# A one-core encoder layer: score corrections over all 128 rows with zeros, and weight chunks placed by their use

## The chip, the cores and the metric

The kernel runs on one core of a Trainium2 chip. A core has TensorE (PE), VectorE (DVE), ScalarE (ACT), GpSimd (POOL) and SyncE (SP), each with its own instruction stream, and they meet through semaphores. The metric is the device time of one execution, in microseconds. All that is told of the hardware here is read from this kernel's trace.

## The reference

The reference is one layer of a hybrid encoder on x of 512 positions by 1024 channels, all in float32. One projection gives q, k, v for differential attention (8 heads, two softmax maps each) and z, x, B, C, dt for a Mamba-2 scan in both directions (16 heads, 4 groups). Both results are concatenated, projected, added to the residual and normalized; then a SwiGLU of width 2816 and a second norm follow.

```python
h = x @ w_in                                    # q, k, v, z, xbc, dt
s = einsum(q, k) * scale - slopes * dist        # two maps c per head
p = softmax(s); a = p[:, :, 0] - lam * p[:, :, 1]
mix = concat(rmsnorm(a @ v), ssd(z, xbc, dt)) @ w_out
x = layernorm(alpha * x + mix)
x = layernorm(alpha * x + (silu(x @ w_gate) * (x @ w_up)) @ w_down)
```

## The kernel before

PE multiplies in float32r. Each float32 operand is split in two parts, h (the value rounded by a copy on ACT) and l (the rest, a subtraction on DVE), and `mm3` (line 174) takes three products: h h, h l, l h. The 130 weight chunks of 128 x 1024 pass through a ring: `wload` brings one by DMA into one of three raw buffers, `wprep` (line 101) makes its two parts `wh` and `wl`, `wget` keeps two chunks ahead. The output projection's and the down projection's last four chunks stay resident (`hold`, `keep`) instead.

Which operand moves differs by stage. For q, k and the convolved columns (`col_units`) the chunk is the stationary operand and x^T (`xh`, `xl`) moves, 512 columns at a time. For z and v (`row_units`) x^T is stationary and the chunk moves, 256 columns at a time. In the SwiGLU, a 2 x 2 Winograd scheme per pair of column tiles (`p_1` to `p_7`, 12 products of 256 columns each, line 887), the weights are stationary; blocks A11 and A12 come from the ring, the sums S1 to S4 and A22 from other tiles. In the output and the down projection the chunk moves, 512 columns.

The stages follow each other: a start (loading and splitting x, dt and decays, first convolution), the scan of four SSD groups into which z and the next group's projections are woven, the attention of eight heads into which the next projections are woven by the hand-written counts HEAD_FILL, the output projection, the norm, the SwiGLU, the down projection. PE's order within a stage is made from this by a scheduler; the listing does not show it.

A head's scores work thus. Q's parts are stacked in `QS`: for map c=0 rows 0 to 63 hold the h part and rows 64 to 127 the l part, for c=1 the other way. `KS` holds K's h part twice, so one product over 128 rows gives Qh Kh + Ql Kh (line 590). What is missing is Qh Kl: `kl` holds K's l part on rows 0 to 63 for c=0 and on 64 to 127 for c=1, and the correction (line 592) multiplies only the 64 rows where QS has the h part. There are 8 heads x 4 tiles x 2 maps = 64 scores and 64 corrections. Each map has its own score bank, two in all. After both, DVE adds the distance penalty and takes a minimum (line 595), ACT the exponential (line 598), then transposes and the product with v follow.

Of the kernel before, what the change touches and what calls it, by code (L numbers as in the profile page):

```python
# [8 lines left out]
F32 = mybir.dt.float32  # L9
# [4 lines left out]
P = 128  # L14
# [36 lines left out]
def encoder(ctx, tc, xt, xs, wall, wdt, consts, masks, vecs, pvec, lnv, out):  # L51
# [21 lines left out]
    def weave(steps, units, counts):  # L73
        """Emits steps in order with counts[i] of the units after step i, and the remaining units at the end."""
        done = 0
        for f, n in zip(steps, counts, strict=True):
            f()
            for u in units[done:done + n]:
                u()
            done += n  # L80
        for u in units[done:]:
            u()

# [1 line left out]
    cst = cp.tile([P, N_C], F32, name="cst")  # L85
# [6 lines left out]

    wcache = {}
    AHEAD = 2

    def wload(i):
# [4 lines left out]
    def wprep(i, raw=None, h=None, l=None):  # L101
        raw = wload(i) if raw is None else raw
        if h is None:
            h = wp.tile([P, 1024], R32, tag="wh", name=f"wh{i}")
            l = wp.tile([P, 1024], R32, tag="wl", name=f"wl{i}")
        A.copy(h, raw)  # L106
        V.tensor_tensor(l, raw, h.bitcast(F32), op=ALU.subtract)  # L107
        wcache[i] = (h, l)
# [6 lines left out]

# [1 line left out]
    xh = xtp.tile([P, KT, S], R32, tag="xh", name="xh")  # L117
# [6 lines left out]
    with tc.tile_pool(name="xraw", bufs=1) as xr:  # L124
# [30 lines left out]
        for k in range(KT):  # L155
            T.matmul(dps[0:32], wdp[:, k], xh[:, k], start=False, stop=False)
            T.matmul(dps[0:32], wdp[:, k], xl[:, k], start=False, stop=k == KT - 1)
        dts = ep.tile([32, S], F32, name="dts")
        A.copy(dts, dps[0:32])
# [21 lines left out]
    def col_units(i, name, done, step=2):  # L181
        """x @ w for 128 columns, transposed: [columns, 512]; then done(psum)."""
        st = {}

        def unit(k0):
            if k0 == 0:
                st["o"] = bank("mm", name)
                st["w"] = [w.rearrange("p (k c) -> p k c", k=KT) for w in wget(i)]
            h, l = st["w"]
            mm3(st["o"], [(h[:, k], l[:, k], xh[:, k], xl[:, k]) for k in range(k0, k0 + step)],  # L190
                first=k0 == 0, last=k0 + step == KT)
            if k0 + step == KT:
                done(st["o"])
        return [lambda k0=k0: unit(k0) for k0 in range(0, KT, step)]

    def row_units(i, name, tag, done):
        """x @ w for 256 columns: two banks of [128 positions, 2, 256]; done(half, psum)."""
        st = {}

        def unit(tp, tt, kh):  # L200
            if (tp, tt, kh) == (0, 0, 0):
                w0, w1 = wget(i, 2), wget(i + 1, 1)
                st["w"] = [[w.rearrange("p (k c) -> p k c", k=4) for w in ww] for ww in (w0, w1)]
            if (tt, kh) == (0, 0):
                st["o"] = bank(tag, f"{name}{tp}")
            t = 2 * tp + tt
            sl = slice(t * P, (t + 1) * P)
            h, l = st["w"][kh]
            mm3(st["o"][:, tt * 256:(tt + 1) * 256],
                [(xh[:, 4 * kh + k, sl], xl[:, 4 * kh + k, sl], h[:, k], l[:, k]) for k in range(4)],  # L210
                first=kh == 0, last=kh == 1)
            if (tt, kh) == (1, 1):
                done(tp, st["o"])
        return [lambda a=(tp, tt, kh): unit(*a) for tp in range(2) for tt in range(2) for kh in range(2)]

# [1 line left out]
    sps = ExitStack()  # L217
# [27 lines left out]

# [1 line left out]
    dtv = ep.tile([P, 2, NT, NH], F32, name="dtv")  # L247
    ex = ep.tile([P, 384], F32, name="ex")
    dd = ep.tile([P, 2, 64], F32, name="dd")
    lhsE = ep.tile([P, S], R32, name="lhsE")  # L250
    vals = ep.tile([P, S], F32, name="vals")
    sel = msk[:, M_SEL:M_SEL + 256].rearrange("p (a k) -> p a k", a=2)
    # per direction d: rows erow[d] carry the exponents, the other 64 rows the mask
    erow = (slice(0, 64), slice(64, 128))
# [8 lines left out]
    def decay_steps(dp):  # L263
# [50 lines left out]

        def s1():
            cum = bank("ps", "cum")
            dAf = dA.rearrange("p d t h -> p d (t h)")
# [52 lines left out]

    # stationary parts of the exponents per direction and half of the columns, in the last mix tiles' places
    lhsC = [[mxp[0].tile([P, NT, P], R32, tag=f"m{q}{14 + d}", name=f"lhsC{d}{q}") for q in "hl"] for d in range(2)]
# [6 lines left out]

    # mix^T in two float32r parts: 16 tiles of [128 channels, 512]  # L380
    mixh, mixl = [None] * 16, [None] * 16
# [6 lines left out]

# [1 line left out]
    bc = lambda a, n: a[:, :, None].broadcast_to([a.shape[0], 4, n])  # L390
# [124 lines left out]

# [1 line left out]
    va, qk = {}, {}  # L517

# [9 lines left out]
    def qk_units(h):  # L528
        i = 24 + 6 * (h // 2) + 2 + 2 * (h % 2)
        QS = qp_[h % 2].tile([P, 2, S], R32, tag="QS", name=f"QS{h}")  # L530
        KS = qp_[h % 2].tile([P, 2, S], R32, tag="KS", name=f"KS{h}")
        kl = qp_[h % 2].tile([P, S], R32, tag="kl", name=f"kl{h}")
        qk[h] = (QS, KS, kl)
# [7 lines left out]
        def kdone(o):  # L541
# [4 lines left out]
            for a, b, c in sides:  # L546
                V.tensor_tensor(kl[a], o[a], KS[a, c].bitcast(F32), op=ALU.subtract)
        return col_units(i, f"q{h}", qdone) + col_units(i + 1, f"k{h}", kdone)

# [1 line left out]
    late = []  # L551
# [18 lines left out]

# [1 line left out]
    mxp[0] = mxs.enter_context(tc.tile_pool(name="mxa", bufs=1, side="right"))  # L572

    def head_steps(h, ap):
# [11 lines left out]
        def scores(t):  # L586
            sl = slice(t * P, (t + 1) * P)
            sbs = [bank("s", f"s{h}{t}{c}") for c in range(2)]
            for c in range(2):
                T.matmul(sbs[c], QS[:, c, sl], KS[:, c], start=True, stop=False)  # L590
            for c, r in enumerate((lo64, hi64)):
                T.matmul(sbs[c], QS[r, c, sl], kl[r], start=False, stop=True)  # L592
            for c, sb in enumerate(sbs):
# [51 lines left out]

# [1 line left out]
    def pair(i, ahead=None):  # L647
        return [w.rearrange("p (k c) -> p k c", k=2) for w in wget(i, ahead)]

    def outer_units(i0, order, lhs, acc, n0, n1, total):  # L650
        """acc(t) += lhs tiles (pairs in order) x weight chunks i0 + n0 .. i0 + n1 - 1."""
        st = {}
# [46 lines left out]

# [1 line left out]
    fx = ctx.enter_context(tc.tile_pool(name="fx", bufs=1))  # L701
# [62 lines left out]
    def tile_major(i0, order, lhs, acc, done, hold, after):  # L764
        """As outer_units, with the last NHELD chunks resident and used one sequence tile at a time."""
        n = len(order)
# [21 lines left out]
    acc1 = [[(bank("ps", f"wo1{t}"), 0, 512)] for t in range(NT)]  # L788
    with tc.tile_pool(name="hw", bufs=1) as hw:
        ln1 = ln_consts(hw, 0)  # L790
        tile_major(I_OUT + 8, OUT_ORDER, mix, acc1.__getitem__, done1,
                   lambda j: [hw.tile([P, 1024], R32, tag=f"{q}{j}", name=f"hold{q}{j}") for q in "hl"],
                   lambda: wget(I_FF))
    mxs.close()

# [1 line left out]
    hidp = ctx.enter_context(tc.tile_pool(name="hid", bufs=1, side="right"))  # L797
# [11 lines left out]

    # Winograd's 2 x 2 form: operands from x1^T's blocks B (k half, sequence half)  # L810
    def block(i, j):
# [16 lines left out]
    def t_steps(q):  # L828
        """x1^T of sequence tile 2 + q, and the operands that come of it."""
        b12, b22 = x1t(2 + q, 0), x1t(2 + q, 1)  # L830
# [12 lines left out]

    # operands from the weight blocks of two column tiles: A11 A12 / A21 A22 (columns, k half)
    ops, mats = {}, {}
# [50 lines left out]
    def put(j, f, c, src):  # L896
        """One block of gate (silu) or up (times gate) into hid."""
        d = hid_tile(f)[:, c]
# [46 lines left out]

    # the first two tiles of gate and up, whole; sequence half 0 of three chunks first
    def ff_w(f, w):
# [50 lines left out]

# [1 line left out]
    NEARLY = 1  # L1000
# [5 lines left out]
    def hid_split(e, ph):  # L1006
        """hid tile e in two parts; the later tiles' parts stay for both column halves."""
        key = e if e >= NRING else (ph, e)
# [39 lines left out]
    ffs.close()  # L1048
    dn = ctx.enter_context(tc.tile_pool(name="dn", bufs=1))
    ln2 = ln_consts(dn, 2)  # L1050
    for f in units[NMORE:]:
# [93 lines left out]
```

## Time and profile before

| | us |
|---|---|
| median of 3 runs | 878.93 |
| lowest, highest | 878.69, 879.1 |
| span of the profiled execution | 876.8 |
| PE busy | 862.4 |
| DVE busy | 616.6 |
| ACT busy | 457.7 |
| POOL busy | 121.3 |

The profile gives the span from the first to the last instruction, and no other time of its own execution; the median lies 2.1 us above it. By the timeline the scores run from 237.8 to 443.0 us, the SwiGLU's blocks from some 552 to 752 us. Products overlap in the record: a product of 512 columns is recorded with some 0.39 us, but the next one starts 0.23 us later. To read what a product costs, take the start of one and the start of the next.

### The profile page before, as it was taken

What the parts mean: (1) busy time and instruction counts of PE and PEld (TensorE: products, weight loads), DVE (VectorE), ACT (ScalarE), POOL (GpSimd) and SP (SyncE); (2) the same over time, 40 slices, a digit from 0 to 9 for tenths busy, and PEclk for the clock granted to TensorE, in tenths of its full rate; (3) what the DMA queues carried; (4) which work ended last, traced back from release to release, by engine and by line L of the source; (5) the groups of instructions that cost most, each with busy time, mean ns of one, the idle gap of its engine ahead of it and who ended that gap; (6) DMA issues with size and microseconds to landing.
All of it is one profiled execution on the core that took longest, in us unless ns stands there. A gap on an engine that the chain in (4) does not pass through costs nothing.

```text
span 876.8 us, 13791 instructions
## 1 busy us (share of the span) xinstructions
PE 862.4 (98%) x5404; PEld 748.6 (85%) x5404; DVE 616.6 (70%) x1071; ACT 457.7 (52%) x893; POOL 121.3 (14%) x137
## 2 busy tenths in 40 slices
PE   7999999999999999999999999999999999999996
PEld 3888989899778687786788889999999999888885
DVE  4978788786567666766644579988888887733617
ACT  4777776667456555655632314555555555621500
POOL 3025252535400000000000023000000000000002
PEclk9999999999999999999999999999999999999999
DMA  7321212112212103111135600343233233332402
GB/s 259 113 96 49 73 50 80 66 49 70 76 49 72 50 25 96 50 49 49 49 109 186 209 25 25 112 129 98 96 123 118 98 116 133 112 96 96 145 1 96
DMA packets 23008, 78.74 MB, mean 90 GB/s; under 512 B 2688, under 2 KB 2944, under 8 KB 22944
## 3 DMA queue, kind: packets, MB, share of 16 engines
q1 hardware_dynamic: 22320, 75.60, 25.8%
q0 software_dynamic: 624, 2.27, 0.8%
q8 instruction: 42, 0.69, 0.3%
q14 instruction: 22, 0.18, 0.1%
HBM read 75.77 MB, written 2.10 MB: 89 GB/s over the span
## 4 chain that ended last, share of the span: by engine, by line
PE 67%; DVE 4%; ACT 1%; issue 1%; DMA 0%; POOLq 0%; POOL 0%; DVEq 0%; ACTq 0%
PE M L887 12%; PE N L887 6%; PE dn L178 4%; PE dn L177 4%; PE dn L179 4%; PE wo L177 3%; PE wo L178 3%; PE wo L179 3%; PE C L887 3%; PE o L618 3%; PE s L592 2%; PE s L590 2%; PE at L606 1%; PE v L177 1%; PE k L177 1%; PE q L177 1%
## 5 line engine op out<-in xcount | busy, mean ns | idle before, releaser
L107 DVE TENSOR_TENSOR wl<-wr,wh 128x1024 fp32r<-128x1024 f32 x101 | 124.5, 1233 | 66.8 <-ACT wh L106 63.5
L106 ACT CAST wh<-wr 128x1024 fp32r<-128x1024 f32 x101 | 105.7, 1049 | 77.6 <-PE wo L179 28.6
L598 ACT ACTIVATE ss<-ss,mn 128x512 f32<-128x512 f32 x64 | 46.0, 720 | 25.9 <-DVE mn L595 25.8
L595 DVE CUSTOM_DVE_ANT_0 ss<-s,tab 128x512 f32<-128x512 f32 x64 | 43.2, 688 | 16.4 <-PE s L592 15.8
L178 PE MATMUL dn<-wl,hidh 128*128 128x512 f32 x130 | 51.0, 392 | 0.0
L177 PE MATMUL dn<-wh,hidh 128*128 128x512 f32 x130 | 50.9, 392 | 0.0
L179 PE MATMUL dn<-wh,hidl 128*128 128x512 f32 x130 | 50.6, 389 | 0.0
L893 ACT COPY e<-M 128x256 f32<-128x256 f32 x60 | 22.4, 372 | 43.1 <-PE M L887 43.0
L456 ACT ACTIVATE rE<-vals,msk 64x128 fp32r<-64x128 f32 x128 | 43.0, 391 | 1.0 <-DVE vals L339 0.4
L177 PE MATMUL wo<-wh,mixh 128*128 128x512 f32 x96 | 38.3, 399 | 0.0
L177 PE MATMUL v<-wh,xh 128*128 128x256 f32 x128 | 37.8, 296 | 0.0
L178 PE MATMUL wo<-wl,mixh 128*128 128x512 f32 x96 | 37.6, 392 | 0.0
L179 PE MATMUL wo<-wh,mixl 128*128 128x512 f32 x96 | 37.5, 390 | 0.0
L179 PE MATMUL v<-wh,xl 128*128 128x256 f32 x128 | 36.7, 286 | 0.0
L177 PE MATMUL z<-wh,xh 128*128 128x256 f32 x128 | 36.4, 286 | 0.0
L178 PE MATMUL v<-wl,xh 128*128 128x256 f32 x128 | 36.3, 284 | 0.0
L179 PE MATMUL z<-wh,xl 128*128 128x256 f32 x128 | 36.2, 283 | 0.0
L178 PE MATMUL z<-wl,xh 128*128 128x256 f32 x128 | 36.2, 283 | 0.0
L618 PE MATMUL o<-va,as 128*128 128x128 f32 x256 | 34.0, 275 | 0.1
L724 POOL TENSOR_TENSOR rs<-rs,mhalf 128x1 f32<-128x1 f32 x8 | 12.2, 1525 | 158.6 <-DVE rs L723 158.6
L708 POOL DMA_DIRECT2D ln<-in_lnv x4 | 2.3, 580 | 227.1 <-PE dn L178 208.8
L618 PEld LDWEIGHTS o<-va,as 128*128 128x128 f32 x256 | 31.6, 192 | 0.7 <-ACT osq L621 0.3
(355 smaller groups left out, 2926.6 us busy)
## 6 DMA issues: line engine op xcount, KB each, us to landing
wr<-in_wall SPq DMA_DIRECT2D x130, 512.0 KB, 3.5
xraw<-in_xt SPq DMA_DIRECT2D x8, 256.0 KB, 6.8
xr<-in_xs SPq DMA_DIRECT2D x4, 512.0 KB, 6.3
ln<-in_lnv POOLq DMA_DIRECT2D x4, 512.0 KB, 4.4
out_y<-xr SPq DMA_DIRECT2D x8, 256.0 KB, 2.0
msk<-in_masks SPq DMA_DIRECT2D x1, 490.0 KB, 5.7
cst<-in_consts SPq DMA_DIRECT2D x1, 448.0 KB, 6.7
vec<-in_vecs POOLq DMA_DIRECT2D x1, 168.0 KB, 5.9
```

The lines of the kernel that those rows point to most:

```text
L106: A.copy(h, raw)
L107: V.tensor_tensor(l, raw, h.bitcast(F32), op=ALU.subtract)
L177: T.matmul(o, ah, bh, start=first and i == 0, stop=False)
L178: T.matmul(o, ah, bl, start=False, stop=False)
L179: T.matmul(o, al, bh, start=False, stop=last and i == n - 1)
L456: A.activation(r[d][e, h], vals[e, sls[t]], AF.Copy, scale=hmask[e, 4 * g + h:4 * g + h + 1])
L590: T.matmul(sbs[c], QS[:, c, sl], KS[:, c], start=True, stop=False)
L595: V.tensor_tensor_reduce(out=s, in0=sb, in1=tab[:, 384 - 128 * t:896 - 128 * t], scale=1.0, scalar=3.0e38, op0=ALU.add, op1=ALU.min, accum ...
L598: A.activation(s, s, AF.Exp, scale=-1.0, bias=mn[:, t, c:c + 1], accum_out=Z[:, t, c:c + 1])
L618: T.matmul(o, ats[t][:, kt * P:(kt + 1) * P], vv[:, kt, j * P:(j + 1) * P], start=kt == 0, stop=kt == NT - 1)
L887: T.matmul(o, x[:, k], y[:, k], start=first and n == 0, stop=last and n == 11, skip_group_check=True)
L893: mats[j]["i" + name] = A.copy(e, src)
```

## The change

Two edits come together.

The corrections now cover all 128 rows. `kl` gets a place for each map, 128 rows by 2 by 512, one buffer per parity of the head that stays for the whole attention; the rows that the map does not need are set to zero once, by POOL. The correction then multiplies the whole of QS's slice, the same stationary operand as the score ahead of it, and stands directly behind that score.

The ring's chunks get a place by their use. A ring tile is 1040 instead of 1024 elements long, so that wh and wl tiles lie 64 bytes apart modulo 128, and a chunk starts 16 elements (64 bytes) into one of them: `wfar` is 1 for the chunks of z, v and the SwiGLU, 0 for the rest. Worked out from the built programs: before, x^T's tiles, the ring's and the mix tiles start at 96 modulo 128 bytes, and the S and A22 tiles at 32. After, z's, v's and the SwiGLU's chunks start at 32, the others at 96. Two pads of 16 elements (`hpad`, `dpad`) bring the held chunks and the hid tiles of the down projection to 96. To make room, `dts` and `vals` share a buffer.

```diff
-    wcache = {}
+    wcache, nW = {}, [0]
...
+    def wfar(i):
+
+        if i < 24:
+            return int(i % 6 in (4, 5))
+        if i < I_OUT:
+            return int((i - 24) % 6 in (0, 1))
+        return int(I_FF <= i < I_DN)
...
         if h is None:
-            h = wp.tile([P, 1024], R32, tag="wh", name=f"wh{i}")
-            l = wp.tile([P, 1024], R32, tag="wl", name=f"wl{i}")
+            n = nW[0] % 3
+            nW[0] += 1
+
+            h, l = (wp.tile([P, 1040], R32, tag=f"w{q}{n}", name=f"w{q}{i}", bufs=1)[:, o:o + 1024]
+                    for q, o in (("h", 16 * wfar(i)), ("l", 16 - 16 * wfar(i))))
...
-        dts = ep.tile([32, S], F32, name="dts")
+        dts = ep.tile([P, S], F32, tag="dv", name="dts")[0:32]
...
-    vals = ep.tile([P, S], F32, name="vals")
+    vals = None
...
         def s1():
+            nonlocal vals
+            vals = ep.tile([P, S], F32, tag="dv", name="vals")
...
-        kl = qp_[h % 2].tile([P, S], R32, tag="kl", name=f"kl{h}")
+        kl = kls.get(h % 2)
+        if kl is None:
+            kl = kls[h % 2] = qp_[h % 2].tile([P, 2, S], R32, name=f"kl{h % 2}")
+            for a, c in ((hi64, 0), (lo64, 1)):
+                G.memset(kl[a, c].bitcast(F32), 0.0)
...
-                V.tensor_tensor(kl[a], o[a], KS[a, c].bitcast(F32), op=ALU.subtract)
+                V.tensor_tensor(kl[a, c], o[a], KS[a, c].bitcast(F32), op=ALU.subtract)
...
                 T.matmul(sbs[c], QS[:, c, sl], KS[:, c], start=True, stop=False)
-            for c, r in enumerate((lo64, hi64)):
-                T.matmul(sbs[c], QS[r, c, sl], kl[r], start=False, stop=True)
+                T.matmul(sbs[c], QS[:, c, sl], kl[:, c], start=False, stop=True)
...
     with tc.tile_pool(name="hw", bufs=1) as hw:
+        hw.tile([P, 16], F32, name="hpad")
...
     dn = ctx.enter_context(tc.tile_pool(name="dn", bufs=1))
+    dn.tile([P, 16], F32, name="dpad")
```

With the comments gone, the line numbers move: 590 and 592 become 607 and 608, 177 to 179 become 188 to 190, 106 becomes 117.

On PE, in the attention, a step of head 1 (`s` the two score banks, `v` the woven projection) before:

```order
L590 MATMUL s_2840<-KS_2571,QS_2570 128x512
L590 MATMUL s_2841<-KS_2571,QS_2570 128x512
L592 MATMUL s_2840<-kl_2572,QS_2570 128x512
L592 MATMUL s_2841<-kl_2572,QS_2570 128x512
L177 MATMUL v_2855<-wh_2598,xh 128x256
L178 MATMUL v_2855<-wl_2599,xh 128x256
```

and after:

```order
L607 MATMUL s_2843<-KS_2573,QS_2572 128x512
L608 MATMUL s_2843<-kl_2574,QS_2572 128x512
L607 MATMUL s_2844<-KS_2573,QS_2572 128x512
L608 MATMUL s_2844<-kl_2574,QS_2572 128x512
L188 MATMUL v_2858<-wh_2602,xh 128x256
L189 MATMUL v_2858<-wl_2603,xh 128x256
```

The first map's correction now stands ahead of the second map's score, and both products of a map use the same QS slice. Seventeen of the 32 steps had the two corrections side by side as here; in the others each stood alone behind its score.

On PE, near the start, `px` is a convolved column tile, `cum` and `pe` are the decays' sums, `z` the first products on chunk 4 (`wh_349`). Before:

```order
L178 MATMUL px_273<-xl,wh_143 128x512
L179 MATMUL px_273<-xh,wl_144 128x512
L319 MATMUL cum<-dA,msk 128x64 x4
L320 MATMUL cum<-dA,msk 128x128
L330 MATMUL pe<-msk,W_202 64x128
L331 MATMUL pe<-cst,W_203 64x128
```

and after:

```order
L190 MATMUL px_272<-xh,wl_144 128x512
L188 MATMUL z_454<-wh_349,xh 128x256
L188 MATMUL z_506<-wh_349,xh 128x256
L188 MATMUL px_346<-xh,wh_165 128x512
L189 MATMUL px_346<-xl,wh_165 128x512
L332 MATMUL cum<-dA,msk 128x64 x4
L333 MATMUL cum<-dA,msk 128x128
L343 MATMUL pe<-msk,W_201 64x128
```

The z rows stood behind all of `cum` and `pe` and now stand ahead of them.

On ACT, near the start, `wh` are casts of weight chunks, `ca` and `co` belong to the convolution, `e` and `lu` to dt. Before:

```order
L106 CAST wh_143<-wr_108 128x1024
L288 ACTIVATE e<-na 128x128
L224 ACTIVATE ca_B_264<-pB_239,pv 128x512
L106 CAST wh_165<-wr_112 128x1024
L291 ACT_TABLE_LOAD
L291 ACTIVATE lu<-u 128x128
L106 CAST wh_276<-wr_274 128x1024
L299 ACTIVATE lu<-u 128x128
L106 CAST wh_349<-wr_347 128x1024
L224 ACTIVATE ca_x_304<-px_273,pv 128x512
L321 ACT_TABLE_LOAD
L321 ACTIVATE ex<-cum 128x384
```

and after:

```order
L299 ACTIVATE e<-na 128x128
L117 CAST wh_275<-wr_273 128x1024
L302 ACT_TABLE_LOAD
L302 ACTIVATE lu<-u 128x128
L117 CAST wh_349<-wr_347 128x1024
L235 ACTIVATE ca_x_303<-px_272,pv 128x512
L242 ACT_TABLE_LOAD
L242 ACTIVATE co_B_265<-ca_B_263 128x512
L310 ACT_TABLE_LOAD
L310 ACTIVATE lu<-u 128x128
L334 ACT_TABLE_LOAD
L334 ACTIVATE ex<-cum 128x384
```

Two more table loads stand ahead of `ex`, since an activation of the convolution (`co_B`) came between those of dt.

## Rows read from the trace of the kernel before

**Rows 1.** The page: busy times of the engines; one group of instructions (busy, mean ns).

```profile
PE 862.4 (98%) x5404; PEld 748.6 (85%) x5404; DVE 616.6 (70%) x1071; ACT 457.7 (52%) x893; POOL 121.3 (14%) x137
...
L595 DVE CUSTOM_DVE_ANT_0 ss<-s,tab 128x512 f32<-128x512 f32 x64 | 43.2, 688 | 16.4 <-PE s L592 15.8
```

**Rows 2.** Busy us by stretch (instructions in brackets), granted clock, DMA; attention, SwiGLU.

```profile
core 0: us, PE busy (x) PEld busy (x) DVE busy (x) ACT busy (x) POOL busy (x), PEclk, DMA share, GB/s
...
227.40:433.00 205.60, 205.21 (x1147) 159.19 (x1145) 139.01 (x318) 118.11 (x270) 15.50 (x15) 1.00 0.18 57
560.00:780.00 220.00, 220.00 (x1773) 214.22 (x1772) 182.29 (x279) 122.58 (x204) 1.13 (x2) 1.00 0.35 114
```

**Rows 3.** Timeline of PE, attention: start, length in us, line, out<-operands, shape, count.

```profile
410.39 0.40 PE L179 MATMUL q<-xh,wl 128*128 128x512 f32 x1
410.63 0.39 PE L590 MATMUL s<-KS,QS 128*128 128x512 f32 x1
410.94 0.49 PE L592 MATMUL s<-kl,QS 64*128 64x512 f32 x1
411.37 0.50 PE L177 MATMUL q<-xh,wh 128*128 128x512 f32 x1
411.70 0.40 PE L590 MATMUL s<-KS,QS 128*128 128x512 f32 x1
```

**Rows 4.** Timeline of PE's weight loads, same place; in brackets idle time before.

```profile
410.39 0.19 PEld L590 LDWEIGHTS s<-KS,QS 128*128 128x128 f32 x1
410.94 0.18 PEld L592 LDWEIGHTS s<-kl,QS 64*128 64x128 f32 x1 [0.36 <-issue]
411.37 0.19 PEld L177 LDWEIGHTS q<-xh,wh 128*128 128x128 f32 x1 [0.24 <-issue]
```

**Rows 5.** Timeline of PE, attention, a step with its two corrections side by side.

```profile
330.90 0.61 PE L590 MATMUL s<-KS,QS 128*128 128x512 f32 x2
331.44 0.50 PE L592 MATMUL s<-kl,QS 64*128 64x512 f32 x2
331.87 0.50 PE L177 MATMUL q<-xh,wh 128*128 128x512 f32 x1
332.21 0.39 PE L178 MATMUL q<-xl,wh 128*128 128x512 f32 x1
```

**Rows 6.** Timeline of PE, output projection, on ring chunks and on held chunks.

```profile
470.26 0.39 PE L177 MATMUL wo<-wh,mixh 128*128 128x512 f32 x1
...
473.66 0.39 PE L177 MATMUL wo<-wh,mixh 128*128 128x512 f32 x1
...
503.39 0.39 PE L177 MATMUL wo<-holdh,mixh 128*128 128x512 f32 x1
...
507.59 0.39 PE L177 MATMUL wo<-holdh,mixh 128*128 128x512 f32 x1
```

**Rows 7.** Timeline of PE, SwiGLU, one step: first row of three runs of products.

```profile
569.45 0.28 PE L887 MATMUL M<-T3h,S3h 128*128 128x256 f32 x1
...
570.81 0.28 PE L887 MATMUL M<-x1h,wh 128*128 128x256 f32 x1
...
572.25 0.28 PE L887 MATMUL C<-x1h,wh 128*128 128x256 f32 x1
```

**Rows 8.** Timeline of PE, v projection: first and last of 41 rows.

```profile
208.18 0.28 PE L177 MATMUL v<-wh,xh 128*128 128x256 f32 x1
...
212.98 0.28 PE L178 MATMUL v<-wl,xh 128*128 128x256 f32 x1
```

**Rows 9.** Waits in the attention: who waited for whom, us in all, times, longest.

```profile
PEld s L590 <- ACT KS L545: 3.2, 8, 0.4
```

**Rows 10.** Timeline of all engines near the start.

```profile
26.59 1.00 PE L319 MATMUL cum<-dA,msk 128*128 128x64 f32 x8
26.60 1.04 ACT L106 CAST wh<-wr 128x1024 fp32r<-128x1024 f32 x1
...
28.35 1.28 ACT L321 ACT_TABLE_LOAD   x1
```

More of the change, by code (lines that the diff above doesn't have):

```diff
@@ L514, in scan_steps @@
         return z, steps, tail, tail2
-    va, qk = {}, {}
+    va, qk, kls = {}, {}, {}
     def v_units(hp):
```

## The prediction

> **What bounds the kernel now.** I read the busy times of the page first, then the busy times by stretch, then the timeline of TensorE and of its weight loads. PE is busy 862.4 of 876.8 us [rows 1], and in each of the two long stages it is busy for practically the whole stretch at a granted clock of 1.00, the 2.4 GHz level, with DVE at 139.01 of 205.60 us in the attention and 182.29 of 220.00 us in the SwiGLU [rows 2]. The other engines have room; PE has none. But "busy" is no measure of pace: a product's recorded time (0.39 us for 512 columns) overlaps the next one's, so what a product costs is the distance from its start to the next start. That is the number I read everywhere below.
>
> The common pace: in the output projection fifteen products of 512 columns take 473.66 - 470.26 = 3.40 us, 0.227 each [rows 6]. Against it stand the attention's scores. Around a correction product (L592, stationary and moving operand 64 rows high) the starts go 410.63, 410.94, 411.37, 411.70 [rows 3]: score product, correction and the product behind it take 1.07 us, where three at 0.227 take 0.68. Excess 0.39 us. Why, the weight loads show: the load of a 128-row product starts with the product ahead of it (L590's at 410.39, the start of the q product), the correction's load only at 410.94, with its own product, and the load of the product behind it at 411.37, again with its own [rows 3, 4]. Two loads that usually lie under a running product lie bare. Elsewhere both corrections of a step stand side by side and share the array: from 330.90 to 332.21 is 1.31 us for five products (two scores, two corrections, the next one), against 5 x 0.227 = 1.135, an excess of 0.175 [rows 5]. In the attention's timeline I counted 17 such pairs and 30 lone corrections, 64 in all.
>
> The second finding is the pace of 256 columns. Twelve products on T3 and S3 take 570.81 - 569.45 = 1.36 us, 0.1133 each; the next twelve, on x1h/x1l and a chunk of the weight ring, take 572.25 - 570.81 = 1.44 us, 0.120 each [rows 7]. The v projection goes at the slower pace, 40 products in 212.98 - 208.18 = 4.80 us [rows 8]. I looked up in the built program where the operands lie: the slow ones have moving and stationary operand at the same offset modulo 128 bytes (both 96), the fast ones 64 bytes apart (96 and 32). Both kinds occur in one SwiGLU step on the same tiles x1h and x1l, so the place is what differs.
>
> **The change part by part.** (1) Corrections over 128 rows. 64 products keep their number and their 512 columns, but need no load of another shape. 30 lone ones give 30 x 0.39 = 11.7 us, 17 pairs 17 x 0.175 = 3.0: -14.7 us. The nearest row for the new form is L590 itself, the same shape from the same QS slice, whose load does go ahead [rows 4]. The other end: should the load stay bare, the lone ones gain nothing and each pair loses its overlap, one product of 0.227: +3.9. I take -14.7, since the new product has L590's shape in every respect. The zeros are written once per buffer (four fills on POOL, which is busy 15.50 of 205.60 us in the attention [rows 2]); kl's two subtractions keep their size. Nothing.
>
> The rule that speaks against this part: the Trainium skill, "TensorE: Matmul & The Clock Gate", Part 3 (Packing small matmuls), says that products of few rows should be put into distinct row groups, where they run concurrently. The trace shows that overlap for 17 pairs [rows 5], and shows beside it the bare loads; by the rule alone part 1 would cost the +3.9 us above instead of giving 14.7.
>
> (2) Weight chunks 64 bytes off where they meet 256-column products. z and v have 4 x 96 products each, 768; the SwiGLU's blocks A11 and A12 20 x 24 = 480; the first ff products 144. At 0.120 - 0.1133 = 0.0067 us each: 5.1 + 3.2 + 1.0 = -9.3 us. The last tile's 256-column products of the down projection go the other way (72, from 64 bytes apart to the same): +0.5. For 512 columns the sign is reversed, weakly: 18 products on the held chunks, 64 bytes apart, take 507.59 - 503.39 = 4.20 us, 0.2333 each, against 0.227 [rows 6]. The change puts those 96 at the same offset: 96 x 0.0066 = -0.6. 252 products of the down projection change in the same way; bounds are 0 and 252 x 0.0066 = -1.7, and I take 0, since the only row is of another stage.
>
> The rule that speaks against part 2: the same page of the Trainium skill, Part 2 (step 1, LDWEIGHTS), says that PE reads the moving and the stationary operand through two independent ports, so that loading takes nothing from the running product. By it the place of an operand could not matter, and part 2 would be 0; rows 7 disagree on one kind of operand, and no run here shows yet that moving a tile does it.
>
> (3) The start is reordered: the two z products now stand ahead of `cum`, and ACT has two more table loads, 1.28 us each, ahead of work that others wait for [rows 10]. PE would reach z where `cum` stands now, at 26.59, and z needs the cast that ends at 26.60 + 1.04 = 27.64 [rows 10]. That is +1.05; bounds 0 (the later z and SSD steps absorb it) and +2.6 (both table loads on the path). I take +1.1.
>
> (4) What the waits take back. PE does wait, in places that its busy share hides: its loads for scores sat idle for KS copies 8 times, 3.2 us [rows 9]. Where z and v run, in the SSD and in the attention, they are the filling between steps whose results come from ACT and DVE; shorter filling lengthens such waits. Bounds: 0 and all of z's and v's 5.1 us. I take half, +2.5. The SwiGLU's and part 1's gain I leave whole: the DVE has 38 us left in the SwiGLU and 67 us in the attention [rows 2].
>
> Sum: -14.7 - 9.3 + 0.5 - 0.6 + 1.1 + 2.5 = -20.5 us on a span of 876.8. The median of the runs, 878.93, lies 2.1 us above that span and I let it stay so: 878.9 - 20.5 = 858.4.
>
> **The rivals.** A, the placement does nothing (0.0067 us belongs to something else in those products): parts 2 and 4 go, -14.7 + 1.1 = -13.6, 865.3 us. For it: no row shows one tile in both places. Against it: rows 7, on the same x1h. By the ports rule of the Trainium skill this is what would come out; the trace disagrees so far.
>
> B, the waits take over in the attention: with the corrections out of the way PE is ahead of the chain add/min, exponential, transposition, and half of the attention's gain (14.7 + half of 5.1, 17.3) goes into waits, of which 1.3 is in part 4 already: 858.4 + 8.6 - 1.3 = 865.7. For it: the KS waits [rows 9]. Against it: DVE would stand at 139 of some 190 us.
>
> C, the load stays bare after all and the pairs lose their overlap: +3.9 for -14.7, 858.4 + 18.6 = 877.0.
>
> D, the one that ends slower: every step of the scores waits for one more add/min. PE writes the two score banks in another order now, and takes its instructions in order; if the second bank is free one row L595 later than needed (0.688 us [rows 1]) in each of 32 steps, that is 22.0 us: 858.4 + 22.0 = 880.4. It decides from 20.5 / 32 = 0.64 us per step on. Against it: the second bank is now needed later than before, behind the first correction.
>
> **How the numbers follow.** Forecast 0.74, A 0.11, B 0.10, C 0.03, D 0.02. The forecast's own range: down 1.7 (down projection), 1.1 (start) and 2.5 (waits) to 853; up 1.5 (start at 2.6) and 2.6 (waits at 5.1) to 862.5. A and B lie at 865 to 866, so 853 to 866 leaves out C, D and tails of the rest. A measurement of this kernel can tell about 0.2%, 1.8 us, from no change: faster by more than that is the forecast, A, B and half of C, 0.965; within it the other half, 0.015; slower 0.02.
>
> **What would show it.** Part 1: L592's successor with a mean near 0.39 us instead of the 0.49 of [rows 3], its loads a product ahead, and score, correction and next product 0.68 us apart; the attention some 16 us shorter. Part 2: z, v, C and M on the weight ring with 0.113 us from start to start; the SwiGLU 3 us shorter. Part 3: z's first rows a microsecond behind `cum`'s old place. Wrong would be unchanged distances with all moved tiles (A), gaps ahead of L590's successor that name ACT or DVE (B), corrections still 0.43 us long (C).

## The result, and the profile after

The changed kernel takes 871.67 us (median of 4 runs, 871.29 to 872.24) beside 878.84 of the kernel before on the same chip: a ratio of 0.9917, 95% interval 0.9903 to 0.9931. That is 7.2 us faster, where 20.5 were forecast; the range of 853 to 866 did not hold it. The profiled execution spans 869.9 us against 876.8.

The page of the changed kernel, in the columns of [rows 1]:

```profile
PE 854.8 (98%) x5404; PEld 757.1 (87%) x5404; DVE 615.4 (71%) x1071; ACT 458.1 (53%) x895; POOL 123.8 (14%) x141
```

PE is the bound as before and is busy 7.6 us less. Where these come from is read from three marks, the starts of the first score, of the first product of the SwiGLU's stage (`ff`) and of the last product, each read off PE's timeline:

| us | before | after | difference |
|---|---|---|---|
| first score | 237.76 | 239.09 | +1.3 |
| first score to first `ff` | 290.59 | 277.30 | -13.3 |
| first `ff` to last product | 340.37 | 345.46 | +5.1 |

The rows of the six starts, first before, then after:

```profile
237.76 0.73 PE L590 MATMUL s<-KS,QS 128*128 128x512 f32 x2 [0.26 <-DVE mixl L387]
528.35 0.36 PE L177 MATMUL ff<-x1h,wh 128*128 128x256 f32 x1
868.72 0.28 PE L179 MATMUL dn13ps<-keeph,hidl 128*128 128x256 f32 x1
```

```profile
239.09 0.50 PE L607 MATMUL s<-KS,QS 128*128 128x512 f32 x1 [0.18 <-DVE mixl L400]
516.39 0.36 PE L188 MATMUL ff<-x1h,wh 128*128 128x256 f32 x1
861.85 0.28 PE L190 MATMUL dn13ps<-keeph,hidl 128*128 128x256 f32 x1
```

So the attention gave nearly what the forecast said, and the SwiGLU with the down projection, in which only gains stood, took 5.1 us of it back.

In the attention, PE and its weight loads in the changed kernel answer to [rows 3] and [rows 4] (start, length, line, product):

```profile
400.95 0.39 PE L607 MATMUL s<-KS,QS 128*128 128x512 f32 x1
401.17 0.39 PE L608 MATMUL s<-kl,QS 128*128 128x512 f32 x1
401.40 0.39 PE L188 MATMUL q<-xh,wh 128*128 128x512 f32 x1
401.63 0.39 PE L607 MATMUL s<-KS,QS 128*128 128x512 f32 x1
```

```profile
400.95 0.19 PEld L608 LDWEIGHTS s<-kl,QS 128*128 128x128 f32 x1
401.18 0.19 PEld L188 LDWEIGHTS q<-xh,wh 128*128 128x128 f32 x1
401.40 0.19 PEld L607 LDWEIGHTS s<-KS,QS 128*128 128x128 f32 x1
```

Score, correction and next product take 401.63 - 400.95 = 0.68 us, as forecast to the hundredth, where the lone correction of [rows 3] had 1.07. The correction's load starts at 400.95, with the score ahead of it, and the load behind it at 401.18, with the correction: none lies bare.

The SwiGLU's step that answers to [rows 7], first row of three runs of twelve products and of what follows them:

```profile
557.54 0.28 PE L904 MATMUL M<-T3h,S3h 128*128 128x256 f32 x1
...
558.95 0.28 PE L904 MATMUL M<-x1h,wh 128*128 128x256 f32 x1
...
560.37 0.28 PE L904 MATMUL C<-x1h,wh 128*128 128x256 f32 x1
...
561.78 0.28 PE L904 MATMUL M<-x1h,A22h 128*128 128x256 f32 x1
```

Here is the surprise. The products on the moved chunks went from 0.120 to 1.42 / 12 = 0.118 us, not to 0.113; and those on T3 and S3, whose operands the change does not mention and which took 0.1133 in [rows 7], take 1.41 / 12 = 0.1175. The output projection on ring chunks, [rows 6] with fifteen products at 0.227, now has (fifteen products again)

```profile
459.10 0.40 PE L188 MATMUL wo<-wh,mixh 128*128 128x512 f32 x1
...
462.60 0.40 PE L188 MATMUL wo<-wh,mixh 128*128 128x512 f32 x1
```

3.50 / 15 = 0.233 us each, although chunk and mix tile are "at the same offset" modulo 128 as before.

### The profile page after: what moved, and what is told of

Read it like the earlier page. It is cut to its first block, busy times and chain, and to the rows that moved or that the text cites. A ratio compares the mean times of both kernels' runs of the same rounds, so it can differ in the third digit from the quotient of the medians.

```text
span 869.9 us, 13803 instructions
## 1 busy us (share of the span) xinstructions
PE 854.8 (98%) x5404; PEld 757.1 (87%) x5404; DVE 615.4 (71%) x1071; ACT 458.1 (53%) x895; POOL 123.8 (14%) x141
## 4 chain that ended last, share of the span: by engine, by line
PE 66%; DVE 4%; issue 1%; ACT 1%; DMA 0%; POOLq 0%; POOL 0%; DVEq 0%; ACTq 0%
PE M L904 13%; PE N L904 6%; PE dn L188 4%; PE dn L190 4%; PE dn L189 4%; PE wo L188 3%; PE wo L189 3%; PE wo L190 3%; PE o L634 3%; PE C L904 3%; PE s L607 2%; PE s L608 2%; PE at L622 1%; PE k L188 1%; PE k L190 1%; PE k L189 1%
```

## The experiments

Two theories stood at first. **P**: the new places of the operands are what slows the SwiGLU. **Q**: places don't matter, and PE's pace sags for some other reason. Places below are modulo 512 bytes, written (moving, stationary).

### One part alone: e1, e2

e1_corr_only has the corrections and the shared `dts`/`vals` buffer on the old ring:

```diff
+            kl = kls[h % 2] = qp_[h % 2].tile([P, 2, S], R32, name=f"kl{h % 2}")
...
+                T.matmul(sbs[c], QS[:, c, sl], kl[:, c], start=False, stop=True)
```

> Part 1 alone: corrections over 128 rows, weight ring, pads and chunks as in the kernel before. In the change the attention gave 13.6 us, the start cost 2.0, the SwiGLU lost 3.9 where 3.2 of gain were forecast. Theory P (the new places are what slows the SwiGLU): here its products go at the old mix, 113 ns on S/T tiles and 120 on ring chunks, and the whole takes 878.8 - 13.6 + 2.0 = 867. Rival Q (the places don't matter; PE's pace sags in the SwiGLU because less idle time stands ahead of it): all its products go at 117 to 118 ns as in the change, and the whole takes 872 to 873.

e2_place_only is the change with the 64-row corrections put back:

```diff
-                T.matmul(sbs[c], QS[:, c, sl], kl[:, c], start=False, stop=True)
+            for c, r in enumerate((lo64, hi64)):
+                T.matmul(sbs[c], QS[r, c, sl], kl[r], start=False, stop=True)
```

> Part 2 alone: ring tiles of 1040 elements, chunks placed by use, pads; corrections over 64 rows as before. P (places slow the SwiGLU by 3.9 us, and give 1.1 in z and v): 878.8 + 3.9 - 1.1 = 881 to 882, SwiGLU products all at 117 to 118 ns. Q (places don't matter, the sag comes from part 1): SwiGLU at 113 and 120 ns, 878 to 879. The forecast's own reading (far chunks at 113 ns): 878.8 - 8 = 871.

Measured: e1 866.82 us (ratio 0.9858, 0.9841 to 0.9874), e2 884.24 (1.0057, 1.0042 to 1.0072). The corrections alone give 12.4 us, the placement alone costs 5.0. By the three marks e1 has +1.9, -14.0, +0.3, and e2 -0.5, +0.5, +4.8. The recorded length of a product tells its pace as well (283 ns recorded is 120 from start to start, 280 is 118, 276 is 113). The C products on ring chunks, grouped by line and shape (count, then busy us and mean ns of one, idle us), of e1 and of e2:

```profile
L892 PE MATMUL C<-x1h,wh 128*128 128x256 f32 x80 | 22.6, 283 | 0.0
```

```profile
L901 PE MATMUL C<-x1h,wh 128*128 128x256 f32 x80 | 22.4, 280 | 0.0
```

P holds and Q falls: the slow SwiGLU comes with the placement, whatever the attention does. P's number for e1, 867, is met; e2 lies 2 us above P's 881 to 882. The two parts add up: -12.4 and +5.0 make -7.4, and the change measured -7.2.

### Which move does it: e3, e4

```diff
-            return int(i % 6 in (4, 5))
+            return 0
...
-        return int(I_FF <= i < I_DN)
+        return 0
```

e3_all_near shifts no chunk, with tiles of 1040 elements and both pads kept; e4_ff_near changes only the last line.

> The change with no chunk shifted (ring tiles and pads stay, every chunk at 96 modulo 128 bytes like x), the order of instructions is the change's. P, if it is the chunk's shift that counts: SwiGLU back at 113 ns on S/T and 120 on ring chunks, z and v at 120: 871.7 - 3.9 + 1.1 = 869. Rival R (what slows is not the shift but the other positions of all tiles): SwiGLU still at 117 to 118, 872 to 873. Q: 872 to 873 as well, told from R by e1_corr_only.

> The change with the SwiGLU's chunks unshifted; z's and v's stay shifted. P with the chunk's shift: SwiGLU at 113/120 again, 871.7 - 3.9 = 868. R and Q: 871.7 as the change, all at 117 to 118.

Measured: e3 872.21 (0.9922, 0.9907 to 0.9937), e4 870.70 (0.9905, 0.989 to 0.992). Against the kernel before on their own chips the change stands at -7.2, e3 at -7.0 and e4 at -8.5 us. Leaving z's and v's shift out (e3 against e4) costs 1.5 us, so it gains that much, not 5.1; leaving the SwiGLU's out (e4 against the change) gains 1.3. The intervals of the three overlap, so these two differences are small beside the noise. The loss itself is still there in e3, 5.4 us behind e1: what slows is not the shift but that **all tiles moved**. A ring tile of 4160 bytes is no multiple of 512. Worked out from the built programs: before, x, ring, T and mix tiles lay at 480 modulo 512, S, A22 and held chunks at 416. In the changed kernel T and mix are still at 480, but x is at 352, S and A22 at 288, and the near chunks lie at 96, 224, 352 or 480 by their slot. All of these agree modulo 128 with what the forecast listed.

### A place by itself: b1

3360 products behind the end of the kernel before, in stretches of 24, each at one pair of places (one execution was taken, so each pair was read once or a few times):

```diff
+    for m in (256, 288, 320, 352, 480):
+        for s in range(256, 512, 32):
+            stretch(512, m, s, name="r")
```

> The kernel before, and behind its end some 3360 more products that nothing reads (the output is not touched by them): stretches of 24 products in the kernel's own pattern (three per pair of h and l parts), on tiles filled with activations, with no other engine at work but in the last sixteen. Each stretch has its moving and its stationary operand at one place modulo 512 bytes. Theory M128 (what the forecast read): 256 columns take 113 ns wherever moving and stationary are 64 bytes apart modulo 128, 120 where they are at the same offset. Theory M256 or wider: 113 ns at (480, 416), 120 at (480, 480), and 118 at (480, 288) and (352, 288), the pairs that the changed kernel has in its SwiGLU. Theory T (what slows is traffic of other engines on the moved tiles, not the place): with nothing beside it the pairs (480, 288), (352, 288) and (480, 416) all take the same 113 ns, and only the stretches beside copies of ACT, subtractions of DVE or loads are slower, by some 5 ns.

First and last row of stretches of 512 columns at (352, 352), (352, 480) and (480, 480); the two letters count places in steps of 32:

```profile
1232.60 0.39 PE L177 MATMUL rll<-bmh,bsh 128*128 128x512 f32 x1
...
1237.82 0.40 PE L179 MATMUL rll<-bmh,bsl 128*128 128x512 f32 x1
...
1254.85 0.40 PE L177 MATMUL rlp<-bmh,bsh 128*128 128x512 f32 x1
...
1260.22 0.39 PE L179 MATMUL rlp<-bmh,bsl 128*128 128x512 f32 x1
...
1299.55 0.39 PE L177 MATMUL rpp<-bmh,bsh 128*128 128x512 f32 x1
...
1304.77 0.39 PE L179 MATMUL rpp<-bmh,bsl 128*128 128x512 f32 x1
```

23 steps take 5.22, 5.37 and 5.22 us: 0.2270, 0.2335, 0.2270 each. (352, 480) is 128 apart, the same place modulo 128, and still slow. All five pairs at the same place took 0.227 to 0.228, the other 35 took 0.229 to 0.234. That fits wo's loss, and q's, k's and the convolution's in the changed kernel, though not every pair of places that these have was among the forty.

256 columns gave no such table. The same pair (480, 288) in two stretches, early and late:

```profile
1039.69 0.28 PE L177 MATMUL ppj<-bmh,bsh 128*128 128x256 f32 x1
...
1042.32 0.28 PE L179 MATMUL ppj<-bmh,bsl 128*128 128x256 f32 x1
...
1389.63 0.28 PE L177 MATMUL unpj<-bmh,bsh 128*128 128x256 f32 x1
...
1392.34 0.28 PE L179 MATMUL unpj<-bmh,bsl 128*128 128x256 f32 x1
```

2.63 / 23 = 0.114 and 2.71 / 23 = 0.118: one place, two paces. (480, 416), which ran at 0.113 in the kernel before, took 0.118 here; (480, 224), 256 bytes apart, and (480, 320), 160 apart, took 0.120 like (480, 480). M128 falls. T falls too: the last sixteen stretches, four each beside ACT's copies, DVE's subtractions, loads and nothing, by stretch of time (columns as in [rows 2]):

```profile
1349.00:1361.00 12.00, 12.00 (x104) 12.00 (x104) 0.00 (x0) 10.55 (x11) 0.00 (x0) 1.00 0.00 0
1361.00:1372.00 11.00, 11.00 (x96) 11.00 (x95) 10.26 (x10) 1.38 (x2) 0.00 (x0) 1.00 0.01 1
1372.00:1384.00 12.00, 12.00 (x104) 12.00 (x103) 2.19 (x4) 0.00 (x0) 0.00 (x0) 1.00 0.71 260
1384.00:1395.00 11.00, 11.00 (x95) 11.00 (x95) 0.00 (x0) 0.00 (x0) 0.00 (x0) 1.00 0.01 4
```

ACT busy 10.55 of 12 us, DVE 10.26 of 11, loads at 260 GB/s, or nothing: PE starts 8.6 to 8.7 products a microsecond in each.

### Nothing moved but the chunks: e5, e5b, e6

Tiles of 1152 elements keep every other tile at its place modulo 512; the raw ring pays for the room with one buffer of three:

```diff
+            h, l = (wp.tile([P, 1152], R32, tag=f"w{q}{n}", name=f"w{q}{i}", bufs=1)[:, o:o + 1024] for q in "hl")
...
+        return 112 * (I_FF <= i < I_DN)
```

> The kernel before, corrections over 64 rows, with the chunks placed by use but nothing else moved modulo 512 bytes: ring tiles are 1152 elements (4608 bytes, a multiple of 512), z's and v's chunks start 64 bytes, the SwiGLU's 448 bytes (64 below the next multiple) into theirs. To make room the raw ring has two buffers instead of three. So x, mix, S, T and all near chunks stay at their old places modulo 512; z and v read (moving, stationary) at (32, 480), the SwiGLU's chunks at (480, 416), as its S tiles in the kernel before. Theory W (places work, but modulo 512 and not 128: the change failed because its 4160-byte tiles moved every other tile): z, v, C and the M's of the ring go at 113 to 114 ns, the 512-column products stay at 227, and the time is 879.2 - 5.1 - 4.2 = 870, plus what the missing raw buffer costs. Theory H (113 ns is a state into which the alternation of product and weight load falls by chance of its history, not one that a place gives): z, v and C at 117 to 118, which is 2 to 3 ns better than 120: 876 to 877. If M and N on S tiles also leave 113, slower than before.

> As e5_place_512, with the sign of the distance exchanged: z's and v's chunks 448 bytes into their tiles (moving 416, stationary 480), the SwiGLU's 64 bytes (480, 32). If only the amount of 64 bytes matters, as in W: 870 again. If the direction matters: z, v, C at 118 or 120 where e5_place_512 has 113, 876 to 879.

> The placement of e5_place_512 together with the corrections over 128 rows, and the pad that puts the held chunks at mix's place (480 modulo 512). By W: 866.8 (corrections alone) - 9.3 - 0.6 = 857, what the forecast had meant. By H: 866.8 - 2.5 = 864. The lost raw buffer may take up to a few microseconds of either.

Measured: e5 884.72 (1.0067, 1.0052 to 1.0082), e5b 883.01 (1.0055, 1.0038 to 1.0072), e6 872.16 (0.9924, 0.9904 to 0.9944): all three miss every number. From the first to the last M, C or N product PE takes 198.43 us in the kernel before, 206.13 in e5, 203.21 in e5b. In e5b that is waiting, for `evac` (a copy out of the bank by ACT), 5.8 us where the kernel before has 0.4 (who waited for whom, us, times, longest; e5b, then before):

```profile
PE M L895 <- ACT e L901: 5.8, 7, 2.4
```

```profile
PE M L887 <- ACT e L893: 0.4, 1, 0.4
```

e5 waits 2.4 there, and the pace below makes some 4 us more (an estimate: 1200 products at 0.118 for 0.113, 480 at 0.118 for 0.120). The third raw buffer is what these kernels lack, but no run puts it back alone, so that the waits come from it is likely and not shown. The paces can be read all the same. C products of e5, then of e5b:

```profile
L895 PE MATMUL C<-x1h,wh 128*128 128x256 f32 x80 | 22.4, 280 | 0.0
```

```profile
L895 PE MATMUL C<-x1h,wh 128*128 128x256 f32 x80 | 22.1, 276 | 0.0
```

In e5, with chunks at (480, 416), everything in the SwiGLU runs at 118, the S products too, which have not moved at all since the kernel before. In e5b, with chunks at (480, 32), everything runs at 113. W falls: the S products have one place in three kernels and two paces.

### The history: b2

```diff
+    for name, places in (("low", [LOW] * 12), ("lowsame", [LOW, SAME] * 6), ("lowhigh", [LOW, HIGH] * 6),
...
+        for s in places:
+            group(name, s)
```

> The kernel before, and behind its end some 1800 more products that nothing reads: groups of 12 of 256 columns in the SwiGLU's own pattern, moving operand always at 480, stationary at 416 (low), 480 (same) or 32 (high), in twelve successions of groups. Theory H (the pace of a place depends on what ran ahead of it): low alone (low, highlow, samelow, twolow) at 118 in long rows, but low in turn with same at 113 / 120 (before's SwiGLU), low in turn with high at 113 throughout (e5b_place_512_swap's), though the low groups have the same places in all of them. Theory W (a place has its pace): low groups at one pace, 113 or 118, in all rows.

The h h products of seven successions (least, median and greatest ns, first and last start):

```profile
L177 PE MATMUL low<-bmh,bsh x48: 280/280/582, 877.1 to 896.0; 128*128 128x256 f32 x48
L177 PE MATMUL lowsame<-bmh,bsh x48: 276/280/283, 896.3 to 912.8; 128*128 128x256 f32 x48
L177 PE MATMUL lowhigh<-bmh,bsh x48: 276/276/276, 913.2 to 929.2; 128*128 128x256 f32 x48
L177 PE MATMUL highlow<-bmh,bsh x48: 276/276/276, 945.8 to 961.8; 128*128 128x256 f32 x48
L177 PE MATMUL same<-bmh,bsh x48: 283/283/283, 962.1 to 979.1; 128*128 128x256 f32 x48
L177 PE MATMUL samelow<-bmh,bsh x48: 276/276/276, 979.4 to 995.4; 128*128 128x256 f32 x48
L177 PE MATMUL highsame<-bmh,bsh x48: 276/282/283, 995.7 to 1012.4; 128*128 128x256 f32 x48
```

`low` and `samelow` are the same 144 products at (480, 416). The first, begun from idle, stays at 280 ns, a pace of 118, for as long as it lasts (its first products, up to 582 ns, began at a granted clock of 0.70 on the mean of 877 to 884 us; from 884 on it is 1.00). The second, begun behind `same`, keeps 276, a pace of 113: it starts at 979.4 and the next succession at 995.7, 16.3 / 144 = 0.113. In `lowsame` the low groups stand at 118 until one `same` group has run, and at 113 from then on. With `high` it is the reverse: in `highsame` the first group stands at 113, and at 118 behind each `same`. H holds in its main point; its details (highlow, samelow and twolow at 118) miss: all three went at 113, behind stretches that ended at 113 or at the same place. So 113 and 118 are two states of one stretch of products, and in these rows a stretch at one place keeps the one in which it entered (b2, too, is one execution).

### The better version: e7, and its control e9

One ring tile whose six parts lie 4096 bytes apart, shifted as a whole while the SwiGLU's chunks are in it, with the corrections and `hpad`:

```diff
+        return 2048 * s + 16 * (I_FF <= i < I_DN)
...
+                wcache["ring"] = wp.tile([P, 6272], R32, tag="ring", name="ring", bufs=1)
+            h, l = (wcache["ring"][:, o + c:o + c + 1024] for c in (0, 1024))
```

e9_corr_ff_low has 112 for the 16, and not an instruction else.

> Corrections over 128 rows (as e1_corr_only), the held chunks at mix's place, and of the placement only this: while the SwiGLU's chunks are in the ring they start 64 bytes higher, at (480, 32); the ring is one tile whose chunks lie 4096 bytes apart, used downwards as the SwiGLU begins and upwards as it ends, so that the shift needs 64 bytes in all, the raw ring keeps its three buffers, and every other tile keeps its place modulo 512. If the distance of +64 beside the S tiles' -64 gives 113 ns, as in e5b_place_512_swap's trace: 624 products x 0.0067 = -4.2, held chunks -0.6, on 866.8: 862. If that pace was only a gift of e5b's waits, SwiGLU products at 118: 866.8 + 3 = 870.

> e7_corr_ff_high with one number changed: the SwiGLU's chunks start 448 instead of 64 bytes higher, so that they lie at (480, 416), where the S tiles lie, and not at (480, 32). Same instructions in the same order, three raw buffers. Theory H (with all operands at low the SwiGLU falls into 118 ns and nothing takes it out): some 1700 products x 4.5 ns = 7.7 us slower than e7, 871, with M and N on unmoved T and S tiles at 118 as well. Theory W (a place has its pace, low was 113 in the kernel before): 863.

Measured: e7 863.33 (0.9817, 0.9804 to 0.9831). e9 869.77 (0.9871, 0.9841 to 0.9901), and its six executions fall into two groups: 861.78 and 863.25, against 869.69, 869.85, 870.12 and 870.36. The same program is as fast as e7 or 7 us slower. One of the four longer executions was profiled, and its SwiGLU goes at 0.118; that the two shorter ones had theirs at 0.113 fits their times, but they left no trace. e7's five lie within 862.20 to 863.52. The SwiGLU of e7 at the moment in which it changes state:

```profile
556.91 0.28 PE L907 MATMUL M<-T3h,S3h 128*128 128x256 f32 x1
...
558.32 0.28 PE L907 MATMUL M<-x1h,ring 128*128 128x256 f32 x1
...
559.68 0.28 PE L907 MATMUL C<-x1h,ring 128*128 128x256 f32 x1
...
561.04 0.28 PE L907 MATMUL M<-x1h,A22h 128*128 128x256 f32 x1
```

T3 and S3 still go at 1.41 / 12 = 0.1175, as in the changed kernel. With these chunks at (480, 32) the pace falls to 1.36 / 12 = 0.1133 and stays there; the median of later S products, unmoved, is 113. It is not the place alone that turns it: the step before, products on chunks at (480, 32) still went at 1.41 / 12:

```profile
549.84 0.28 PE L907 MATMUL C<-x1h,ring 128*128 128x256 f32 x1
...
551.25 0.28 PE L907 MATMUL M<-x1h,A22h 128*128 128x256 f32 x1
```

The same rows as at the turn in e9, chunks at (480, 416), in an execution of the longer group:

```profile
558.39 0.28 PE L907 MATMUL M<-x1h,ring 128*128 128x256 f32 x1
...
559.81 0.28 PE L907 MATMUL C<-x1h,ring 128*128 128x256 f32 x1
```

1.42 / 12 = 0.118. H's number for e9 was 871, with the execution that was profiled at 870.36; that some executions take the other state was not foreseen. Even this execution begins its M, C and N products at 0.1133 (from 540.80 to 542.16 us, twelve products at (480, 416)) and goes at 0.118 from 546.44 us on, behind a gap of 0.2 us between two products. What decides which state a stretch takes, and why e9 does not turn back as e7 does, is open.

### The start: e8, e10, e11

```diff
+            with tc.issue_after(cums[-1].ins):
...
+                with tc.issue_after(lus[-1].ins):
+                    A.activation(r, a, AF.Tanh)
```

e8_start_order has the lower hunk, e10_z_behind_cum the upper (around z's and v's products), e11_both both, all on e7.

> e7_corr_ff_high, with the convolution's first tanh held behind dt's second logarithm on ACT, so that one table load of 1.28 us less stands ahead of ex (three in all instead of four); the two z products stay ahead of cum on PE. If the table loads are what the start lost (term 3 of the forecast, measured +2.0 to the first score in e1_corr_only), this gives 1.3 to 2 us: 861.3 to 862. If the z products ahead of cum are the cause, nothing: 863.3.

> e7_corr_ff_high, with the z products held behind cum on PE; the four table loads stay ahead of ex on ACT. If z's wait on its cast (0.95 us in e1_corr_only's timeline) is what counts: 863.3 - 1 = 862.3. If the sums cum and pe have to wait for ACT's table loads anyway: 863.3.

> e7_corr_ff_high, with both: z behind cum, and the first tanh behind dt's second logarithm (three table loads). cum, pe and z then stand in the order of the kernel before. If the start's loss is the order of these: 863.3 - 2 = 861.3. If it is neither: 863.3, and the start's loss lies elsewhere.

Measured: 862.42, 863.18 and 862.78 us; their intervals against the kernel before (0.9798 to 0.9823, 0.9811 to 0.9838, 0.9806 to 0.9833) overlap e7's. Neither the table load nor z's place is the start's 2 us. e11 does not quite restore the old order: two px products still stand ahead of `cum`, and z runs only from 42.35 us, where it ran from 29.75. Its first score starts at 239.83, as late as in e1 (239.64), and PE stands idle once for 1.7 us ahead of the second convolved column:

```profile
28.07 0.47 PE L191 MATMUL px<-xh,ring 128*128 128x512 f32 x1 [1.68 <-DVE u L315]
```

It waits there for dt's chain on DVE, and the traces show where that chain is late. dt's first exponential on ACT (`e`), before and in e1:

```profile
20.87 0.31 ACT L288 ACTIVATE e<-na 128x128 f32<-128x128 f32 x1 [1.99 <-DVE na L287]
```

```profile
22.83 0.30 ACT L288 ACTIVATE e<-na 128x128 f32<-128x128 f32 x1
```

In e1 ACT runs the convolution's `ca_B` (21.21) and a cast (21.89) ahead of it, in the kernel before behind it. `e` starts 1.96 us later, and `cum`, which needs what comes of it, at 28.64 instead of 26.59. In all ten traces with corrections over 128 rows, e8, e10 and e11 among them, `e` starts 2.02 to 2.07 us behind the end of `na`, the DVE step whose result it takes; in all six with 64 rows it starts 0.03 to 0.04 behind it. No run put `e` back alone, so this cause is read from the traces and not tested. (The mark of the first score itself differs between executions: in b2, which has the start of the kernel before, it stands at 239.18.)

## Why the prediction was wrong

**Term 1, the corrections: right.** -14.7 us were forecast; in e1, between the first score and the first `ff`, -14.0 came. 0.68 us from score to next product, the loads a product ahead, DVE and ACT able to follow: each of its signs is in the rows above. C is out, and B: with the whole 14 us gone from PE no wait takes them back. D too: in the attention of the changed kernel the loads for scores waited for the add and minimum seven times, 1.6 us in all, not 22.0; DVE itself still waits for the corrections, 5.7 us in all where [rows 1] has 15.8.

```profile
L611 DVE CUSTOM_DVE_ANT_0 ss<-s,tab 128x512 f32<-128x512 f32 x64 | 42.7, 683 | 5.9 <-PE s L608 5.7
```

**Term 2, the placement: this is the step that failed.** -9.3 (with +0.5 and -0.6, -9.4) were forecast, e2 measured +5.0: 14.4 us apart, more than the 13.3 by which the whole was missed. The step was "the slow ones have moving and stationary operand at the same offset modulo 128 bytes (both 96), the fast ones 64 bytes apart ... so the place is what differs". Three things were wrong in it.

First, the measure. 128 is the smallest power of two modulo which the two kinds of [rows 7] differ, and it was taken as the true period. b1 shows 128 bytes apart to be another place (0.2335 against 0.2270). With the wrong measure the list of tiles "at 96 before and after" hid that the tiles of 4160 bytes had moved all of them. The question that was not asked: where do the tiles of the tuned kernel lie modulo more than 128? x, ring, T and mix all lie at 480 modulo 512, S, A22 and the held chunks at 416, and the change broke that.

Second, the price was taken from [rows 7] as belonging to the place. b2 shows that at (480, 416) 0.113 and 0.118 both occur, by what ran ahead. In the kernel before, the slow chunks at (480, 480) stood between the S products, and in b2 it is just such a group that turns the following ones to 113. The 480 slow products whose 3.2 us were to be saved went together with the 113 of the 1200 others: e9's longer executions show what it costs when the turn is missed, 7 us. That the 480 products are what turned the others in the kernel before is read from b2; its own trace agrees (M on T2 and S1 takes 1.42 / 12 from 556.27 us, M on A22, behind a later pair of groups at (480, 480), 1.36 / 12 from 564.01), but no run tested it there.

Third, the 512-column products were thought untouched but for the held chunks, "252 products of the down projection" bounded by 0 and -1.7. In the changed kernel most of wo's ring products went from 0.227 to 0.233, with chunks at 96, 224 or 352 against 480. The held chunks' -0.6 did not come either: they lie at 352 against 480 there. In e7 both lie at 480, and 14 products on them take 3.17 us, 0.227 each.

Rival A said what comes of places that do nothing, 865.3; no rival said that they could do harm. The same would follow from the rule of the Trainium skill, "TensorE: Matmul & The Clock Gate", Part 2 (step 1, LDWEIGHTS), that the two operands come through independent ports. b1 disagrees with what follows from it: with nothing else at work, place alone makes 0.2270 or 0.2335.

**Term 3, the start: right in sign, small in size, and by luck.** +1.1 forecast, +1.9 measured in e1 (bound 2.6). It comes with the corrections' part of the edit, since e2 has -0.5; the two causes that the forecast named are not it, by e8, e10 and e11. What the traces show in their place is dt's first exponential, 2 us later behind its input on ACT.

**Term 4, the waits: not found.** +2.5 was set against shorter z and v. These went from 0.120 to between 0.116 and 0.118 (in e3, unshifted, to 0.118 as well), worth some 2 us on 768 products by these paces; in the attention the loads for scores still wait for KS 3.1 us in all, as in [rows 9], so nothing visible was lost there.

Together: +14.4 (term 2), +0.7 (term 1), +0.8 (term 3), -2.5 (term 4) make +13.4; 871.7 - 858.4 is +13.3.

## What to carry to other kernels

Before tiles are moved or padded, list where every operand of the busiest engine lies, modulo more than the distance that seems to matter (here 512 bytes), and keep that: in this kernel a pad of 64 bytes per tile cost more than the best place could give. A pace that is read at one spot of a trace belongs to that spot with all that runs ahead of it; a price per instruction that rests on place should be measured on the moved tiles, or in a stretch by itself, before it is multiplied by hundreds. And when two edits come as one, each by itself tells at once which of them works: the corrections alone were better than both by 5 us, and with a shift that moves nothing else they reach 863.3.

## What the runs showed of the hardware that was not expected

- 512 float32r columns start every 0.227 us when moving and stationary operand lie at the same place modulo 512 bytes, and every 0.229 to 0.234 at the 35 other pairs of places tried, with nothing else at work (b1); copies, subtractions and loads of other engines beside 256-column products change nothing in these stretches.
- 256 columns have three paces: 0.120 at the same place (in b1 also at some places 160 or 256 bytes apart), and 0.113 or 0.118 at most others. At one and the same place both of these occur, a run of products can keep its pace for 144 of them, and a group at another place can turn it (b2).
- One program can therefore have executions of two lengths at the same granted clock: e9 at 862 to 863 and at 870 us.
